# A one-core encoder layer: RWKV inverses solved in place through one scratch tensor, DVE block transposes, score pieces of four chunks, and stores issued by ACT

## The chip, the cores and the metric

The kernel runs on one core of a Trainium2 chip. A core has five engines that run at the same time, each with its own instruction stream in program order: TensorE (PE; PEld is its weight load), VectorE (DVE), ScalarE (ACT), GpSimd (POOL) and SyncE (SP). DMA transfers are issued by SP, by POOL or by ACT, and an instruction that issues one stands in that engine's queue like any other. The metric is the device time in microseconds of one execution.

## The reference

One layer of a "hybrid streaming encoder" on a prompt of 1,024 rows and a sample of 64 rows, width 1,024. One input projection of 9,864 columns feeds three token mixers and the gates:

```python
cols = x @ lw['w_in'] + lw['b_in']
ya, shift1, wkv1 = rwkv7_branch(a_cols, ...)     # A: 8 heads x 64, delta-rule state
yb, conv1, c1, n1, m1 = mlstm_branch(b_qk, ...)  # B: 4 heads x 128, matrix memory
yc = stick_breaking(c_q, kc, vc, k_past, v_past) # C: 8 heads x 64, attention without softmax
br = einsum('btnc,ncd->btnd', [ya*silu(a_z), yb*silu(b_z), yc*silu(c_z)], w_branch)
mix = sum(sigmoid(gates) * br, axis=2) @ w_out
x = layer_norm(DEEPNORM_ALPHA * x + mix)
x = x + (p @ w_ple) * sigmoid(x @ w_ple_gate)
```

Branch A is the recurrence `S = S*w_t + (S @ -kk_t) (kk_t*a_t)^T + v_t k_t^T`, `y_t = S @ r_t`. The kernel does it in chunks of 64 rows. Within a chunk the effect of the rows on each other is the inverse of a 64x64 unit triangular matrix, one for each head and chunk.

## The kernel before, in words

**Two kinds of work.** `main` computes the input projection in blocks of 128 columns, each in three row groups (384, 384, 320). A block is 72 matmuls: eight pieces of the inner dimension, three products each, since an fp32 number is split into two parts (`xh`, `xl` for x, `whl` for the weights). ACT or DVE evicts a group from one of three PSUM banks into one of four stages, and `store` writes the stage to DRAM (`xsd`, `brd`, `crd`, `bo`, `yz`, `gt`). The blocks stand in the order A, gates of B, B, C, then the silu and merge gates. `main` ends with `m_begin` (L1007), which waits until C is done and the first branch is converted for the merge (`m_prep`, `yconv`); then come the merge (three branches of eight blocks, `bk<-heapr,whl`) and the tail (`w_out`, layer norm, `w_ple`).

Beside it runs `side`: the three mixers one after the other. `a_all` does eight fronts (four pairs of heads, two halves of 8 and 9 chunks), `b_all` begins when the last front is done, and `c_all` when B is done. C's products have operands in the `heapr` buffer alone (`bk<-heapr`), and their evictions go to ACT and DVE.

**What sets the order.** A planner (`Sched`, L125) runs while the program is built. It keeps a clock for each engine and a price for each instruction, and takes a side task's next instruction as soon as its inputs are ready by these clocks; in between it emits `main`'s matmuls. The result is one fixed order for each engine. `get` (a piece of the heap) holds a task until the heap has room, and `bank` until a PSUM bank is free.

**The way of one RWKV half.** `a_front` (L1332) makes scores: `SC` holds, for each chunk, two 64x64 triangles (the one to invert, and the one for the output), `UV` the values; both are taken for the whole half and given back at the end of `a_chain`. At its end it writes the four 32x32 diagonal blocks of the pairs to the scratch `nd`, eight DMAs with 128-byte runs (L1480 to L1486). `a_inverse` (L1495) loads them as N, one block to a partition (two DMAs, 4 KB a partition), sets Q to the identity, and for j from 31 to 1 does two products on POOL: `tm = N[:, j] * Q[j, :]`, `Q -= tm`. DVE makes a transposed copy of the upper blocks in N (L1518), and Q and N go to the scratches `qd` and `xd`. `a_corner` (L1526) brings them back in ten DMAs with 128-byte runs, and makes the off-diagonal block of each inverse by two small products on TensorE (32x32, `bk<-heap,heap 32*32`) with ACT between. `a_chain` (L1573) then walks through the chunks one by one. Only one inverse and one corner run at a time.

All of these DMAs, the stores of `main` and the weight loads are issued by SP, in order.

## Time and profile before

| what | value |
|---|---|
| time, median of 3 runs | 1,891.88 us (1,881.05 to 1,899.76) |
| the profiled execution's own time | 1,887.65 us |
| its span, first to last instruction | 1,885.9 us |
| mean granted TensorE clock | 0.973 |
| POOL, DVE, ACT busy | 30%, 62%, 42% |
| DMA packets | 212,280, of them 41,592 under 512 B |

The profile is of one execution. The page has the busy time of each engine, the span in 40 slices of 47 us (a digit is tenths of busy time), the chain of work that ended last, and groups of instructions by line. Rows of a stretch give, for each engine, its busy time and in brackets the count of its instructions, then the granted clock (1.00 is full speed), the share of the DMA engines and GB/s. A row of a group reads: line, engine, operation, out<-in with shapes, count | busy us, mean ns of one | idle time before it and what ended it. Rows of DMA issues (`SPq`) give the least, median and largest time that the queue spent on one issue, and when the first and last began. A line such as L353, L358 or L427 is that of a helper (`act`, `tt`, `dma`) which many places call; in the changed kernel these below L384 are the same and the others four higher.

### The profile page before, as it was taken

The page shows a single profiled execution, that of the slowest core. Times are in us where ns is not written, and L with a number is a line of the kernel's source. Part 1 is how long each engine was busy: PE and PEld are TensorE (multiplying, and loading weights), DVE is VectorE, ACT ScalarE, POOL GpSimd, SP SyncE. Part 2 cuts the span into 40 slices and gives each one's busy share as a digit, 9 for nine tenths or more (in the row PEclk, how much of TensorE's full clock was granted, in tenths as well). Part 3 has the DMA queues.
Part 4 walks back from the last instruction along what each step waited for, and adds up shares of the span by engine and source line. Part 5 has one row for each costly group of instructions (what it writes and reads, how often), then busy time and mean ns, then how long its engine had stood idle before and what let it go on. Part 6 is the DMA issues. An engine that isn't in the chain of part 4 may idle for free.

```text
span 1885.9 us, 30250 instructions
## 1 busy us (share of the span) xinstructions
PE 1763.8 (94%) x10873; PEld 1619.1 (86%) x10873; DVE 1178.7 (62%) x2588; ACT 784.9 (42%) x1781; POOL 556.9 (30%) x1028
## 2 busy tenths in 40 slices
PE   6999999989999999999999999999966799988999
PEld 5999888979898899999999999999844799866787
DVE  8346466564647554756876266666666678888643
ACT  5444444344444344545444354645453222211321
POOL 6007445362617522810611221212020000345100
PEclk9999999999999999999999999999977899989999
DMA  4323423223232332343633442423211877522321
GB/s 148 109 83 87 112 71 95 80 83 109 77 92 67 110 85 77 99 119 114 198 122 115 141 125 68 116 90 110 72 53 35 264 229 232 158 90 78 125 80 60
DMA packets 212280, 206.55 MB, mean 110 GB/s; under 512 B 41592, under 2 KB 180650, under 8 KB 212130
## 3 DMA queue, kind: packets, MB, share of 16 engines
q1 hardware_dynamic: 207338, 191.86, 33.4%
q0 software_dynamic: 4704, 12.71, 2.1%
q8 instruction: 86, 1.41, 0.3%
q14 instruction: 64, 0.52, 0.1%
q10 hardware_dynamic: 88, 0.04, 0.0%
HBM read 136.25 MB, written 68.34 MB: 108 GB/s over the span
## 4 chain that ended last, share of the span: by engine, by line
PE 41%; issue 8%; DVE 8%; ACT 2%; POOL 2%; DMA 1%; SPq 0%; POOLq 0%; DVEq 0%; ACTq 0%
PE bk L321 39%; PE bk L328 3%; DVE heap L376 2%; DVE heap L397 2%; DVE heap L358 2%; DVE heapr L358 1%; POOL heap L414 1%; ACT heapr L353 1%; ACT heap L353 1%; DMA heap<-yz 1%; DMA heap<-gd 0%; DVE whl L358 0%; DVE heap L408 0%; POOL heap L419 0%; ACT whl L353 0%
## 5 line engine op out<-in xcount | busy, mean ns | idle before, releaser
L321 PE MATMUL bk<-xh,whl 128*128 128x384 f32 (+3 forms) x3792 | 1065.9, 342 | 0.3 <-DVE heap L376 0.3
L321 PEld LDWEIGHTS bk<-xh,whl 128*128 128x128 f32 (+1 forms) x3792 | 685.0, 188 | 11.9 <-issue 3.0
L321 PE MATMUL bk<-xl,whl 128*128 128x384 f32 (+3 forms) x2184 | 674.7, 330 | 1.7 <-POOL xl L360 1.2
L321 PEld LDWEIGHTS bk<-xl,whl 128*128 128x128 f32 (+1 forms) x2184 | 406.0, 189 | 6.0 <-POOL xl L360 1.8
L353 ACT ACTIVATE heap<-bk 64x64 f32<-64x64 f32 (+10 forms) x639 | 216.4, 346 | 433.1 <-PE bk L321 143.9
L360 POOL TENSOR_TENSOR heap<-heap 32x31 f32<-32x31 f32 (+33 forms) x514 | 347.0, 675 | 159.4 <-DMA heap<-nd 121.2
L328 PE MATMUL bk<-ident,heap 128*128 128x128 f32 (+3 forms) x942 | 184.7, 293 | 57.1 <-DVE heap L376 18.5
L358 DVE TENSOR_TENSOR whl<-heap,whl 128x1024 fp32r<-128x1024 f32 (+1 forms) x114 | 122.8, 1078 | 147.8 <-ACT whl L353 121.8
L328 PEld LDWEIGHTS bk<-ident,heap 128*128 128x128 f32 (+3 forms) x942 | 125.3, 149 | 82.3 <-DVE heap L376 21.4
L358 DVE TENSOR_TENSOR heap<-heap 128x256 f32<-128x256 f32 (+18 forms) x376 | 186.4, 501 | 13.6 <-DMA heap<-yz 2.8
L321 PE MATMUL bk<-heap,heap 128*128 128x128 f32 (+3 forms) x1360 | 170.6, 255 | 18.7 <-ACT heap L353 16.6
L321 PEld LDWEIGHTS bk<-heap,heap 128*128 128x128 f32 (+2 forms) x1360 | 142.9, 162 | 46.2 <-ACT heap L353 31.6
L353 ACT ACTIVATE heap<-bk,pc 128x384 f32<-128x384 f32 (+5 forms) x218 | 114.3, 547 | 137.4 <-PE bk L321 102.0
L321 PE MATMUL bk<-heapr 128*128 128x256 f32 (+2 forms) x524 | 131.0, 355 | 12.1 <-DVE heapr L358 5.6
L376 DVE SCALAR_TENSOR_TENSOR heap<-heap 128x4 f32<-128x4 f32 (+9 forms) x265 | 106.0, 402 | 50.4 <-ACT heap L353 45.0
L321 PE MATMUL bk<-heapr,whl 128*128 128x384 f32 (+2 forms) x648 | 119.6, 343 | 18.8 <-ACT heapr L353 18.5
L353 ACT ACTIVATE heap<-heap 64x64 f32<-64x64 f32 (+9 forms) x328 | 111.0, 343 | 61.5 <-DVE heap L376 20.1
L353 ACT ACTIVATE whl<-heap 128x1024 fp32r<-128x1024 f32 (+1 forms) x116 | 105.4, 910 | 68.0 <-PE bk L321 58.9
L321 PEld LDWEIGHTS bk<-heapr,whl 128*128 128x128 f32 x648 | 110.6, 192 | 25.2 <-ACT heapr L353 20.3
L321 PEld LDWEIGHTS bk<-heapr 128*128 128x128 f32 x524 | 89.4, 202 | 29.8 <-DVE heapr L358 12.1
L397 DVE TENSOR_TENSOR_SCAN heap<-heap,cst 128x128 f32<-128x128 f32 (+8 forms) x68 | 96.3, 1420 | 28.2 <-POOL heap L414 16.2
L353 ACT ACTIVATE heap<-bk,hb 128x384 f32<-128x384 f32 (+1 forms) x120 | 67.5, 563 | 109.5 <-PE bk L321 88.9
(153 smaller groups left out, 1808.4 us busy)
## 6 DMA issues: line engine op xcount, KB each, us to landing
heap<-in_w_in_dram SPq DMA_DIRECT2D x77, 512.0 KB
heap<-gt SPq DMA_DIRECT2D x24, 544.0 KB
gt<-heap SPq DMA_DIRECT2D x48, 192.0 KB
heap<-in_x_prompt_dram SPq DMA_DIRECT2D x16, 512.0 KB
heap<-crd SPq DMA_DIRECT2D x12, 544.0 KB
heap<-yd SPq DMA_DIRECT2D x24, 272.0 KB
heap<-yz SPq DMA_DIRECT2D x24, 272.0 KB
heap<-in_w_branch_dram SPq DMA_DIRECT2D x24, 256.0 KB
```

Of the source, the lines that this page charges most:

```text
L321: lambda: self.nc.tensor.matmul(out, lhsT, rhs, start=start, stop=stop, skip_group_check=more),
L328: lambda: self.nc.tensor.transpose(out, in_, self.ident[:p, :p]), load=(0.82 * fsize(in_), d))
L353: return self.nc.scalar.activation(out, in_, func, **kw)
L358: lambda: self.nc.vector.tensor_tensor(out=out, in0=a, in1=b, op=op))
L360: lambda: self.nc.gpsimd.tensor_tensor(out=out, in0=a, in1=b, op=op))
L376: lambda: self.nc.vector.scalar_tensor_tensor(out=out, in0=a, scalar=s, in1=b, op0=op0, op1=op1))
L397: return self.S.emit("dve", fsize(out) * 1.06 + 65, rd, [out], lambda: self.nc.vector.tensor_tensor_scan(out=out, data0=d0, data1=d1, init ...
L414: return self.S.emit("pool", fsize(out) * 1.0 + 130, [in_], [out], lambda: self.nc.gpsimd.affine_select(out=out, in_=in_, pattern=pattern, ...
```

## The change

Four edits, and one price in the planner:

1. **Pieces.** `SC` and `UV` are taken for four chunks at a time, and given back in `a_chain` as soon as the fourth chunk is through. The triangle to invert is stored with its sign turned (`maskb`), and its whole 64x64 form goes to `nd` as soon as four chunks are scored: four or five DMAs in a half, 256-byte runs, in place of eight.
2. **In place.** N is loaded from `nd` (two DMAs, 128-byte runs in the scratch), gets ones on its diagonal, and is inverted in place for j from 30 to 1; Q, its clearing and `qd`, `xd` are gone. The result goes back to the same places of `nd` (two DMAs).
3. **Block transposes.** `a_corner` fetches whole triangles in four or five DMAs in place of ten, and DVE transposes their upper blocks (`tr32`), in place of the copy on DVE and two loads from `xd`.
4. **Stores.** `raw`, which evicts the blocks of B and C, the output gate and the merge gates, has ACT issue the store right behind its own eviction. The silu blocks (`z`) and A's blocks keep SP.
5. The planner's price of a scan becomes 2.13 ns an element and 90, from 1.06 and 65.

```diff
-HEAP = 17256
+HEAP = 17264
+    def tr32(self, out, in_):
+        return self.S.emit("dve", fsize(out) * 1.06 + 65, [in_], [out], lambda: self.nc.vector.transpose(out, in_))
     def scan(self, out, d0, d1, init, op0, op1):
-        return self.S.emit("dve", fsize(out) * 1.06 + 65, rd, [out], lambda: self.nc.vector.tensor_tensor_scan(
+        return self.S.emit("dve", fsize(out) * 2.13 + 90, rd, [out], lambda: self.nc.vector.tensor_tensor_scan(
...
-            self.store(i_, dst[:, t0:t0 + n], d, done if g == 2 else None)
+            self.store(i_, dst[:, t0:t0 + n], d, done if g == 2 else None, kind != "z")
-    def store(self, i, out, d, done):
+    def store(self, i, out, d, done, now=False):
+        if now:
+            self.dma(out, d, "a")
+            if done:
+                self.have.add(done)
+            return
         self.kept |= {i}
...
-        inv = [self.must(n, True) for n in (1024, 1024, 256, 288)]
+        inv = [self.must(n, True) for n in (1024, 240, 288)]
+        yield self.cp(self.maskb, self.mask[:, :])
+        yield self.ts(self.maskb[:, 64:128], self.mask[:, 64:128], -1.0, OP.mult)
...
-        SC = yield from self.get(nc * 256)
-        UV = yield from self.get(nc * 128)
+        SC, UV = [], []
+        nd = self.dr.tile([9, 2, 64, 64], F32, name="nd", bufs=3)
         for c0 in range(0, nc, 4):
+            SC.append((yield from self.get(m * 256)))
+            UV.append((yield from self.get(m * 128)))
...
             for e in range(min(m, 2)):
+                yield self.dma(nd[c0 + e:c0 + m:2].rearrange("c h s j -> (h s) c j"),
+                               sc4[:, e::2, 0, 64 - 64 * e:128 - 64 * e], "s")
...
-        for k in range(2):
-            for h in range(2):
-                s = slice(64 * h + 32 * k, 64 * h + 32 * k + 32)
-                for e in range(2):
-                    o = 64 - 64 * e + 32 * k
-                    yield self.dma(nd[k, h * nc + e:(h + 1) * nc:2].rearrange("c s j -> s c j"),
-                                   sc4[s, e::2, 0, o:o + 32], "s")
...
+        blk = [nd.rearrange("c h s j -> (c h) s j")[0:B, 32 * k:32 * k + 32, 32 * k:32 * k + 32] for k in range(2)]
-            yield self.dma(N[k * B:(k + 1) * B, :1024], nd[k, 0:B].rearrange("c s j -> c (s j)"), "s")
-        yield self.memset(Q[0:P, :1024], 0.0)
-        yield self.memset(Q[0:P, :1024][:, ::33], 1.0)
+            yield self.dma(rows[k], blk[k], "s")
+        yield self.memset(N[0:P, :1024][:, ::33], 1.0)
-        for j in range(31, 0, -1):
-            w = 32 - j
+        for j in range(30, 0, -1):
+            w = 31 - j
             yield self.tt(t3, n3[:, 0:j, j:j + 1].to_broadcast([P, j, w]),
-                    q3[:, j:j + 1, j:32].to_broadcast([P, j, w]), OP.mult, IE)
-            yield self.tt(q3[:, 0:j, j:32], q3[:, 0:j, j:32], t3, OP.subtract, IE)
+                    n3[:, j:j + 1, j + 1:32].to_broadcast([P, j, w]), OP.mult, IE)
+            yield self.tt(n3[:, 0:j, j + 1:32], n3[:, 0:j, j + 1:32], t3, OP.add, IE)
-        yield self.cp(N[0:B, :1024].rearrange("p (j s) -> p j s", s=32),
-                Q[0:B, :1024].rearrange("p (s j) -> p j s", j=32))
         for k in range(2):
-            yield self.dma(qd[k, 0:B].rearrange("c s j -> c (s j)"), Q[k * B:(k + 1) * B, :1024], "s")
-        yield self.dma(xd[0:B].rearrange("c s j -> c (s j)"), N[0:B, :1024], "s")
+            yield self.dma(blk[k], rows[k], "s")
...
+                yield self.dma(v, nd[cs].rearrange("c h s j -> (h s) c j"), "s")
+        for v, cs in parts:
+            yield self.tr32(x13[:, cs, :], v[:, :, 0:32])
...
                 if c % 4 == 3 or c == 8:
+                    self.free(SC[c // 4], UV[c // 4])
-            self.free(BK, KR, PC, SC, UV)
+            self.free(BK, KR, PC)
```

How this moves instructions, at three places. First TensorE at the end of C, before: projections have `xh,whl`, C's products `heapr` or `ident,heap`, the merge `heapr,whl`. These are the last rows of C and the first of the merge:

```order
L328 MATMUL bk_69<-ident,heap 128x128 x4
L321 MATMUL bk_72<-heapr 128x256
L321 MATMUL bk_68<-heapr 128x256
L321 MATMUL bk_72<-heapr 128x256 x3
L328 MATMUL bk_70<-ident,heap 128x128 x4
L321 MATMUL bk_68<-heapr 128x256 x3
L321 MATMUL bk_72<-heapr 128x256 x4
L321 MATMUL bk_65<-heapr,whl 128x384 x12
```

The same place now, the last products of C:

```order
L321 MATMUL bk_65<-xh,whl 128x384
L321 MATMUL bk_72<-heapr 128x256
L321 MATMUL bk_65<-xh,whl 128x384
L321 MATMUL bk_65<-xl,whl 128x384
L321 MATMUL bk_65<-xh,whl 128x384
L321 MATMUL bk_72<-heapr 128x256 x3
L321 MATMUL bk_66<-xh,whl 128x384
L321 MATMUL bk_66<-xl,whl 128x384
```

Before, 298 products of C stand behind the last projection; now projections stand between them to the last, and 120 behind it.

Second SP around one inverse (the second half of the first pair), before:

```order
L427 DMA qd<-heap 18x1024 x2
L427 DMA xd<-heap 18x1024
L743 DMA heap<-in_w_in_dram 128x8x128
L427 DMA brd<-heap 128x320
L427 DMA heap<-xd 32x9x32
L427 DMA heap_76<-qd 32x5x32
L427 DMA heap<-bond 128x256
L427 DMA heap_76<-qd 32x4x32
L427 DMA heap_76<-qd 32x5x32
L427 DMA brd<-heap 128x384
L427 DMA heap_76<-qd 32x4x32
L427 DMA heap<-xd 32x9x32
```

Such a place now:

```order
L431 DMA nd<-heap 18x32x32
L431 DMA nd<-heap_76 128x2x64
L431 DMA nd<-heap 18x32x32
L431 DMA nd<-heap_76 128x2x64
L431 DMA heap<-nd 128x2x64 x3
L431 DMA heap_76<-xsd 128x576
L431 DMA heap<-nd 16x32x32
L431 DMA heap_76<-xsd 128x576 x2
L431 DMA yd<-heap 128x256
L431 DMA heap<-nd 128x2x64
L431 DMA heap<-nd 128x64
```

Two issues take an inverse out and five bring its triangles back, the next half's pieces and loads stand between, and no store of a projection block (`brd`) does.

Third ACT while C runs, with what each instruction waits for in brackets (`DMAHW4` is one of eight slots that DMAs take in turn), now:

```order
L353 ACTIVATE heap<-bk_66,hb 128x384 [waits DMAHW2_49,PE_49]
L431 DMA gt<-heap 128x384 [waits DMAHW4_49,Activation_49]
L353 ACTIVATE heap<-bk_68 128x128 [waits DVE_49,PE_49]
L353 ACTIVATE heap<-bk_70 128x128 [waits PE_49]
L353 ACTIVATE heap<-bk_71 128x256 [waits PE_49]
L353 ACTIVATE heap<-bk_69 128x256 [waits PE_49]
L353 ACTIVATE heap<-bk_67,hb 128x320 [waits DMAHW5_49,PE_49]
L431 DMA gt<-heap 128x320 [waits DMAHW6_49,Activation_49]
```

The store waits for ACT's own eviction and for an older transfer in its slot, and the evictions of C wait behind it; before, no DMA stood between them.

More of the change, by code (lines that the diff above doesn't have):

```diff
@@ L1315, in a_all @@
                "V2": self.must(128, True), "U2": self.must(128, True), "bn": [self.must(256, True) for _ in range(2)]}
-        inv = [self.must(n, True) for n in (1024, 1024, 256, 288)]
+        inv = [self.must(n, True) for n in (1024, 240, 288)]
         self.bkd = self.must(1024, True)
+        mb = self.must(192, True)
+        self.maskb = mb[:, :192]
+        yield self.cp(self.maskb, self.mask[:, :])
+        yield self.ts(self.maskb[:, 64:128], self.mask[:, 64:128], -1.0, OP.mult)
         lists = ("Z", "ya", "bn")
-        self.ast = [*Z, *cst["ya"], *cst["bn"], *[x for k, x in cst.items() if k not in lists], *inv, self.bkd]
+        self.ast = [*Z, *cst["ya"], *cst["bn"], *[x for k, x in cst.items() if k not in lists], *inv, self.bkd, mb]
         self.bond = self.dr.tile([4, 128, NT], F32, name="bond")
@@ L1451, in a_front @@
             for i, c in enumerate(cr):
-                yield self.stt(sc4[:, c, 0, :], bs[0][:, i * 128:(i + 1) * 128], nsb[:, c:c + 1],
-                               self.mask[:, c % 2 * 64:c % 2 * 64 + 128], OP.mult, OP.mult)
+                yield self.stt(sc4[:, i, 0, :], bs[0][:, i * 128:(i + 1) * 128], nsb[:, c:c + 1],
+                               self.maskb[:, c % 2 * 64:c % 2 * 64 + 128], OP.mult, OP.mult)
             for e in range(min(m, 2)):
-                yield self.tt(sc4[:, c0 + e:c0 + m:2, 1, :],
+                yield self.dma(nd[c0 + e:c0 + m:2].rearrange("c h s j -> (h s) c j"),
+                               sc4[:, e::2, 0, 64 - 64 * e:128 - 64 * e], "s")
+            for e in range(min(m, 2)):
+                yield self.tt(sc4[:, e::2, 1, :],
                               bs[1][:, :m * 128].rearrange("p (a b) -> p a b", b=128)[:, e::2, :],
@@ L1552, in a_corner @@
             for h in range(2):
-                yield self.mm(bs[h][top[h], c * 32:(c + 1) * 32], x13[low[h], c, :], sc4[low[h], c, 0, 96 - c % 2 * 64:128 - c % 2 * 64], True, True)
+                yield self.mm(bs[h][top[h], c * 32:(c + 1) * 32], x13[low[h], c, :], tri(c)[low[h], 32:64], True, True)
         for h in range(2):
-            for e in range(2):
-                yield self.act(sc4[top[h], e::2, 0, 96 - 64 * e:128 - 64 * e],
-                               bs[h][top[h], :nc * 32].rearrange("p (a b) -> p a b", b=32)[:, e::2, :], AF.Copy, scale=-1.0)
+            for v, cs in parts:
+                yield self.act(v[top[h], :, 32:64],
+                               bs[h][top[h], :nc * 32].rearrange("p (a b) -> p a b", b=32)[:, cs, :], AF.Copy)
             self.unbank(bs[h])
@@ L1599, in a_chain @@
             C0, nc_ = (0, 8) if hf == 0 else (8, 9)
-            bk3, kr3, sc4, uv3 = BK.v(nc_, 128), KR.v(nc_, 128), SC.v(nc_, 2, 128), UV.v(nc_, 128)
+            bk3, kr3 = BK.v(nc_, 128), KR.v(nc_, 128)
             for c in range(nc_):
+                sc3, uv2 = (x[c // 4].v(min(4, nc_ - c // 4 * 4), n, 128)[:, c % 4] for x, n in ((SC, 2), (UV, 1)))
+                uv2 = uv2[:, 0, :]
                 if c + C0 == 16:
```

51 lines of the change are left out of this document (24 added, 27 removed).

## The prediction

> **What bounds the kernel now.** I read the page from the top: the busy line, then the slices.
>
> ```profile
> span 1885.9 us, 30250 instructions
> PE 1763.8 (94%) x10873; PEld 1619.1 (86%) x10873; DVE 1178.7 (62%) x2588; ACT 784.9 (42%) x1781; POOL 556.9 (30%) x1028
> PE   6999999989999999999999999999966799988999
> ```
>
> TensorE is busy 94% of the span, so its work sets the time nearly everywhere, and a change to the RWKV branch (POOL, DVE, DMA) can only pay where TensorE is not covered. The slices show two such places before the tail: the start, and slices 29 to 31 (6, 6, 7), around 1,365 to 1,480 us. I then cut the time by stages with the busy time of the engines in chosen stretches:
>
> ```profile
> core 0: us, PE busy (x) PEld busy (x) DVE busy (x) ACT busy (x) POOL busy (x), PEclk, DMA share, GB/s
> 82.00:810.00 728.00, 701.10 (x4721) 654.71 (x4720) 418.12 (x1190) 321.06 (x842) 332.37 (x599) 0.99 0.32 90
> 810.00:1075.00 265.00, 262.47 (x1751) 251.16 (x1750) 166.55 (x483) 117.80 (x301) 62.67 (x128) 1.00 0.42 130
> 1075.00:1150.00 75.00, 73.25 (x467) 68.80 (x466) 49.31 (x56) 43.58 (x81) 17.21 (x48) 1.00 0.41 131
> 1150.00:1361.00 211.00, 206.06 (x1332) 194.38 (x1330) 139.06 (x158) 109.39 (x206) 31.17 (x108) 1.00 0.31 93
> 1361.00:1453.00 92.00, 63.45 (x309) 49.59 (x307) 63.33 (x77) 44.39 (x87) 13.83 (x45) 0.80 0.12 32
> 1453.00:1477.00 24.00, 5.73 (x10) 2.66 (x10) 10.79 (x15) 4.59 (x7) 0.00 (x0) 0.56 0.62 200
> 1477.00:1624.00 147.00, 146.93 (x874) 146.02 (x874) 112.10 (x204) 36.37 (x64) 2.17 (x4) 0.99 0.74 241
> ```
>
> From 82 to 1,361 us TensorE issues one matmul per 0.15 to 0.16 us and stands still for 36 us in all (26.9 + 2.5 + 1.8 + 4.9). From 1,361 to 1,477 it issues 319 in 116 us, at a granted clock of 0.80 and then 0.56. This is one hole, and why it opens is told by the last store of the projections and by who ended TensorE's waits there (first row the stores; the others the waits from 1,361 to 1,477):
>
> ```profile
> L427 SPq DMA_DIRECT2D gt<-heap x72: 319/320/562, 922.5 to 1361.4; - x72
> ```
> ```profile
> PE bk L321 <- ACT heapr L353: 23.6, 14, 6.8
> PE bk L328 <- DVE heapr L358: 10.6, 2, 5.3
> ```
>
> The last projection block leaves at 1,361 us. Until then stick-breaking attention (C) runs between projection matmuls, which fill its waits. After it, 298 products of C stand in TensorE's order with nothing between them (the first excerpt of the order in the section on the change), so each wait for an eviction or a split is bare. Then comes the conversion of the first branch for the merge, bare as well:
>
> ```profile
> 1451.89 0.62 PE L321 MATMUL bk<-heapr 128*128 128x256 f32 x3 [0.34 <-DVE heapr L358]
> 1459.30 1.77 PE L321 MATMUL bk<-heapr,whl 128*128 128x384 f32 x3 [6.79 <-ACT heapr L353]
> ...
> 1476.36 2.09 PE L321 MATMUL bk<-heapr,whl 128*128 128x384 f32 x4 [3.98 <-ACT heapr L353]
> ```
>
> So the bound is TensorE's work plus one hole of 116 us, which exists because C starts too late for the projections to last.
>
> **The main term: C starts earlier.** The change itself does no TensorE work less; counted in the built order, both kernels have 7,984 products ahead of the merge, 5,616 of them projections. What moves is the mixture. Before, 3,471 projection matmuls stand ahead of the last corner product of the RWKV inverses, 4,704 ahead of C's first product, and all 5,616 ahead of its last 298. Now it is 2,517, 3,963, and 5,496 ahead of C's last product: 120 are left behind it. The fronts wait for heap; score pieces that are freed after four chunks let them in sooner, and mLSTM and C follow. The planner's new price for a scan also moves C's rows; it is nearer to the trace, where a scan of 1,024 took 2,277 ns, about 2.2 ns an element:
>
> ```profile
> L397 DVE TENSOR_TENSOR_SCAN heap<-heap,cst 128x1024 f32<-128x1024 f32 x8 | 18.2, 2277 | 0.0
> ```
>
> What do 319 products cost when they are covered? In 1,150 to 1,361 the two mixtures run together:
>
> ```profile
> L321 PE MATMUL bk<-xh,whl 128*128 128x384 f32 (+1 forms) x506 | 143.7, 337 | 0.0
> L321 PE MATMUL bk<-xl,whl 128*128 128x384 f32 (+1 forms) x253 | 83.0, 328 | 0.0
> ```
>
> 506 + 253 = 759 of the 1,332 are projections. A dense row of such matmuls costs 147/874 = 0.168 us (the stretch from 1,477). 759 x 0.168 = 127.5 us; the other 573 products share the remaining 83.5 us, 0.146 us each. The hole holds 309 of C and 10 of the merge: 309 x 0.146 + 10 x 0.168 = 46.8 us. So 116 us become 47: **-69 us**. The smallest saving is where the 69.2 us of busy time there (63.45 + 5.73) do not shrink at the full clock: -47. The largest takes all C products at 0.13 us: -74. I take -69, since the interleaved stretch is the same code doing the same steps.
>
> **What is late next.** The conversion for the merge needs C's buffers free, so it still starts after C. It took from 1,452.5 to 1,477, 24.5 us. The 120 projections behind C cover 120 x 0.168 = 20.2 us, but they bring evictions to ACT and weight splits to DVE, which do the conversion too. I put back **+8 us**: between 24.5 - 20.2 = 4 and half as much again for the conversion, 36.7 - 20.2 = 16.
>
> **The inverse.** Per half it has 60 POOL products instead of 62, over 4,960 elements each way instead of 5,456 (the sums over j of j(31-j) and j(32-j)), and one clearing of 1,024 less.
>
> ```profile
> L360 POOL TENSOR_TENSOR heap<-heap x496: 227/592/2531, 146.8 to 793.9; 32x31 f32<-32x31 f32 x6, 32x112 f32<-32x112 f32 x6, 32x175 f32<-32x175 f32 x6, 32x220 f32<-32x220 f32 x6
> ```
> ```profile
> 466.80:508.20 41.40, 36.50 (x62) 1.00 0.21 64
> 741.20:794.10 52.90, 46.27 (x62) 1.00 0.30 88
> ```
>
> The fifth inverse took 41.4 us of POOL, the last 52.9. At 4,960/5,456 of the work the typical one takes about 38. Eight follow each other on POOL (8 x 38 = 304 us); from the first inverse to the last corner the new order has some 2,440 products (3,524 less 1,087, counted to the corners), at 0.154 us 376 us. That is enough, though with less room. Two small DVE instructions make the negated mask before the branch begins. The copy that transposed one triangle on DVE goes (eight of some 1.1 us), and 36 block transposes come:
>
> ```profile
> L381 DVE COPY heap<-heap 18x1024 f32<-18x1024 f32 x4 | 4.4, 1096 | 0.5 <-POOL heap L360 0.5
> L381 DVE COPY heap<-bk 64x64 f32<-64x64 f32 x68 | 14.8, 218 | 35.5 <-PE bk L321 34.9
> ```
>
> The trace has no block transpose. With 64 elements in a lane it is nearest to the copy of 64 (0.22 us, 8 us in all); like the long copy it would be 39 us. I take 0.22: nothing, since DVE stands idle 43% of 82 to 810 us. Without that cover it is four or five in a row, 1 us, ahead of each corner.
>
> The transfers around an inverse all stand in SP's queue:
>
> ```profile
> L427 SPq DMA_DIRECT2D nd<-heap x64: 302/432/1736, 124.2 to 735.9; - x64
> L427 SPq DMA_DIRECT2D heap<-nd x16: 281/360/1284, 141.2 to 737.7; - x16
> L427 SPq DMA_DIRECT2D heap<-qd x64: 303/431/697, 203.0 to 815.6; - x64
> L427 SPq DMA_DIRECT2D qd<-heap x16: 296/360/413, 198.1 to 794.5; - x16
> L427 SPq DMA_DIRECT2D heap<-xd x16: 303/394/622, 202.4 to 803.3; - x16
> L427 SPq DMA_DIRECT2D xd<-heap x8: 264/300/370, 199.0 to 795.3; - x8
> ```
>
> 184 issues become 104 (36 pieces out, 16 blocks in, 16 back, 36 pieces in). 80 x 0.43 = 34 us of SP's issuing go, 4 us per half. But the blocks now go in and out in runs of 32 numbers (128 B) where they went in runs of 4 KB. Landing can be bounded by the two kinds: 4 KB runs, issued at 144.04 and used by POOL at 146.82; 128 B runs, issued at 215.91 and used by TensorE at 217.96:
>
> ```profile
> 144.04 0.38 SPq L427 DMA_DIRECT2D heap<-nd  x1
> ```
> ```profile
> 146.82 1.33 POOL L360 TENSOR_TENSOR heap<-heap 32x31 f32<-32x31 f32 x4 [6.14 <-DMA heap<-nd]
> ```
> ```profile
> 215.91 0.58 SPq L427 DMA_DIRECT2D heap<-qd  x1
> ```
> ```profile
> 217.96 0.69 PE L321 MATMUL bk<-heap,heap 32*32 32x32 f32 x32
> ```
>
> 2.8 and 2.05 us: no price for the short runs shows. I take 0 net for the inverse, between -4 and +6 us per half of its own latency, which TensorE does not wait for while its order leaves the room.
>
> **Stores from ACT.** 156 stores of 128x384 leave SP (24 blocks of B and C, 28 of two gate kinds, three each). On ACT each costs its issue and a wait for ACT's own eviction to be written (and, in the order, for an older transfer in its slot). The nearest row:
>
> ```profile
> L427 ACTq DMA_DIRECT2D grd<-heap x6: 246/250/271, 208.6 to 217.9; - x6
> ```
>
> 0.25 to 0.32 us (SP's `gt` stores) and as much again for the wait: 156 x 0.5 = 78 us on an ACT that is idle half of 1,150 to 1,361 (109 of 211). Behind a store stand the evictions of C and RWKV, for which TensorE waits, so up to a quarter may show: 0 to +15 us. Against it SP, freed of them, issues loads sooner. I take **0** for ACT and for the denser RWKV stage together, between -8 and +20.
>
> **Sum**, on the profiled execution's own 1,887.65 us (1.75 above its span, 4 below the median of the three runs): 1,887.65 - 69 + 8 = **1,826 us**.
>
> **The rivals.**
> (a) POOL is late: the RWKV stage gets denser, and every inverse runs like the last one (52.9 instead of 41.4). For: that row. Against: TensorE's waits from 82 to 1,361 us name no DMA; the longest is
>
> ```profile
> PE bk L321 <- ACT heap L353: 18.4, 25, 2.2
> ```
>
> and the other four name DVE. If half of the 11.5 us shows at eight corners, 8 x 5.7 = 46: 1,872. The Trainium skill, in "SBUF — State Buffer", section "Who interferes with whom", says that a POOL instruction that reads SBUF and a DVE instruction with two SBUF inputs exclude each other for a whole instruction; the one long inverse would fit that, and no run here isolates it.
> (b) Short runs cost: two 2 us legs more per inverse, bare on TensorE, 8 x 4 = 32: 1,858. Against: the 2.05 us above. The Trainium skill, in "DMA: Bandwidth & Descriptors", section "Specifications", asks for 512 B or more to a piece and says that smaller ones are read, changed and written back; by it (b) would hold, and the trace shows no such price at these counts.
> (c) The hole only moves: C's own chain is slow wherever it runs, and TensorE waits in order among projections. Against: 206 of 211 us busy in 1,150 to 1,361. Then 1,880 to 1,888.
> (d) Slower: ACT stands still at each store until an older transfer lands. A group of projections lasts 24 x 0.168 = 4.0 us; ACT uses 109/211 of it, so 1.9 us are free. A hold of 2.0 to 2.8 us and 0.3 to issue exceeds that by 0.4 to 1.2, say 0.8: 156 x 0.8 = 125, 1,951. It decides from 61/156 = 0.4 us lost per store. Against: the six stores of `grd` that ACT issues now at 0.25 us.
>
> **How the numbers follow.** The forecast 0.80 (its own range 1,800 to 1,850), (a) 0.06, (b) 0.04, (c) 0.05, (d) 0.05. The range, 1,800 to 1,862, spans the forecast's with -74 and the gains in SP at the lower end and reaches over (b). More than 1% is about what a measurement of this kernel can tell from no change. Faster by more: the forecast, (b) and half of (a), 0.87. Within 1%: the rest of (a) and most of (c), 0.08. Slower: (d), 0.05.
>
> **What would show it.** Right: `gt` stores end within some 25 us of C's last product; TensorE's slices at 29 to 31 read 9; granted clock near 1.0 to the merge; one wait of under 15 us before it. POOL products 480, the last inverse done about 120 us earlier. Wrong: TensorE's still time from 82 us to C's end above 60 us, with POOL, DMA or ACT as its releaser; ACT's queue standing over 1 us at stores.

## The result, and the profile after

The changed kernel took 1,791.7 us (median of four runs, 1,787.4 to 1,796.0) beside 1,892.6 us for the kernel before: a ratio of 0.947, 95% interval 0.942 to 0.953. The forecast was 1,826 us, with 1,800 at the lower end of its range. The direction and the place were right; the gain was half as large again as the forecast. The profiled execution took 1,793.5 us, 94 less than the 1,887.65 on which the sum was made, where the forecast was 62 less.

The page of the changed kernel, its span, the busy line of TensorE, the slices and POOL's products:

```profile
span 1791.5 us, 30062 instructions
PE 1719.0 (96%) x10873; PEld 1591.3 (89%) x10873; DVE 1169.2 (65%) x2618; ACT 790.8 (44%) x1821; POOL 511.3 (29%) x1004
PE   6999999999999999999999999999998999978999
L360 POOL TENSOR_TENSOR heap<-heap 32x30 f32<-32x30 f32 (+16 forms) x498 | 312.3, 627 | 37.3
```

TensorE has as many matmuls as before (10,873) and the hole of slices 29 to 31 (counted from 0) is gone: they read 9, 8, 9. Next the stretches, cut where the built order changes: RWKV up to its last chain, mLSTM up to the first product of stick-breaking (C), C among projections, the conversion for the merge, and the rest. No product of C is left without projections, so the bare stretch of before has no counterpart.

```profile
81.00:713.00 632.00, 609.68 (x4266) 555.32 (x4264) 414.81 (x1275) 311.47 (x893) 292.28 (x579) 1.00 0.34 95
713.00:951.00 238.00, 237.31 (x1542) 230.39 (x1542) 149.57 (x421) 111.07 (x258) 48.91 (x116) 1.00 0.44 136
951.00:1353.00 402.00, 402.00 (x2648) 389.19 (x2648) 257.14 (x295) 214.91 (x395) 71.46 (x209) 1.00 0.34 99
1353.00:1389.00 36.00, 29.93 (x167) 28.63 (x166) 15.03 (x22) 10.49 (x18) 0.00 (x0) 0.91 0.72 231
1389.00:1791.00 402.00, 374.99 (x1874) 327.66 (x1872) 282.75 (x495) 100.75 (x182) 67.70 (x41) 0.97 0.43 140
```

From 81 us to C's end TensorE stands still for 22.3 + 0.7 + 0.0 = 23 us. The third row is the surprise: 2,648 products in 402 us without any idle time. The same cut through the kernel before:

```profile
1087.00:1361.00 274.00, 267.31 (x1725) 251.21 (x1722) 183.16 (x209) 144.64 (x277) 47.70 (x153) 1.00 0.33 99
```

There 6.7 us were idle, and a product took 274/1,725 = 0.159 us; now 0.152. The other places that the prediction named, in the changed kernel: the stores of the gates, the waits of TensorE from 1,353 us, the block transposes, and POOL's products of the inverses.

```profile
L431 ACTq DMA_DIRECT2D gt<-heap x72: 326/326/379, 952.4 to 1373.7; - x72
```
```profile
PE bk L321 <- ACT heapr L353: 5.7, 2, 5.1
PE bk L321 <- DVE heapr L376: 0.3, 1, 0.3
```
```profile
L386 DVE STREAM_TRANSPOSE heap<-heap x36: 163/230/246, 197.3 to 650.5; 128x64 f32<-128x64 f32 x32, 128x32 f32<-128x32 f32 x4
```
```profile
120.00:720.00 600.00, 264.72 (x480) 1.00 0.34 97
```

The last store goes 20 us after C's last product, one wait of 5.1 us stands ahead of the merge, a transpose takes 0.23 us, and POOL does 480 products in 264.7 us, 33 us per half.

### The profile page after: what moved, and what is told of

Same layout as the page of the kernel before. It is cut to its first block, busy times and chain, and to the rows that moved or that the text cites. A ratio compares the mean times of both kernels' runs of the same rounds, so it can differ in the third digit from the quotient of the medians.

```text
span 1791.5 us, 30062 instructions
## 1 busy us (share of the span) xinstructions
PE 1719.0 (96%) x10873; PEld 1591.3 (89%) x10873; DVE 1169.2 (65%) x2618; ACT 790.8 (44%) x1821; POOL 511.3 (29%) x1004
## 3 DMA queue, kind: packets, MB, share of 16 engines
q0 software_dynamic: 4704, 12.71, 2.2%
## 4 chain that ended last, share of the span: by engine, by line
PE 81%; DVE 11%; ACT 4%; issue 2%; DMA 2%; ACTq 0%; SPq 0%; POOL 0%; DVEq 0%
PE bk L321 76%; PE bk L328 6%; DVE heap L376 4%; ACT heap L353 3%; DVE heap L358 2%; DVE heap L371 1%; DVE heapr L358 1%; DVE whl L358 1%; DVE heap L412 1%; DMA heap<-in_x_prompt_dram 1%; DVE xl L358 0%; DMA heap<-in_w_ple_dram 0%; DMA out_c_p_dram<-heap 0%; DVE heap L409 0%; ACT whl L353 0%
## 5 line engine op out<-in xcount | busy, mean ns | idle before, releaser
L321 PEld LDWEIGHTS bk<-xh,whl 128*128 128x128 f32 (+1 forms) x3792 | 681.1, 187 | 13.5 <-issue 3.9
L353 ACT ACTIVATE heap<-bk 64x64 f32<-64x64 f32 (+9 forms) x679 | 219.2, 335 | 399.9 <-PE bk L321 137.8
L360 POOL TENSOR_TENSOR heap<-heap 32x30 f32<-32x30 f32 (+16 forms) x498 | 312.3, 627 | 37.3
L328 PE MATMUL bk<-ident,heap 128*128 128x128 f32 (+3 forms) x942 | 177.3, 280 | 36.4 <-DVE heap L376 22.1
L358 DVE TENSOR_TENSOR heap<-heap 128x256 f32<-128x256 f32 (+15 forms) x359 | 176.1, 497 | 16.2 <-DMA heap<-yz 7.8
L358 DVE TENSOR_TENSOR whl<-heap,whl 128x1024 fp32r<-128x1024 f32 (+1 forms) x114 | 121.7, 1069 | 91.2 <-ACT whl L353 87.9
L321 PE MATMUL bk<-heap 128*128 128x128 f32 (+6 forms) x1156 | 169.0, 270 | 10.0 <-ACT heap L353 8.5
L328 PEld LDWEIGHTS bk<-ident,heap 128*128 128x128 f32 (+3 forms) x942 | 120.7, 143 | 55.0 <-DVE heap L376 25.8
L321 PEld LDWEIGHTS bk<-heap 128*128 128x128 f32 (+2 forms) x1156 | 126.6, 163 | 40.6 <-ACT heap L353 21.9
L353 ACT ACTIVATE heap<-heap 64x64 f32<-64x64 f32 (+8 forms) x328 | 111.0, 343 | 63.4 <-DVE heap L376 30.5
L376 DVE SCALAR_TENSOR_TENSOR heap<-heap 128x4 f32<-128x4 f32 (+8 forms) x264 | 100.8, 383 | 55.3 <-ACT heap L353 49.6
L401 DVE TENSOR_TENSOR_SCAN heap<-heap,cst 128x512 f32<-128x512 f32 (+8 forms) x68 | 96.4, 1419 | 45.5 <-POOL heap L418 26.1
L321 PE MATMUL bk<-heapr 128*128 128x256 f32 (+2 forms) x524 | 119.4, 329 | 0.0
L321 PE MATMUL bk<-heap,heap 128*128 128x128 f32 (+3 forms) x788 | 108.2, 263 | 8.3 <-ACT heap L353 6.5
```

The lines of the kernel that those rows point to most:

```text
L321: lambda: self.nc.tensor.matmul(out, lhsT, rhs, start=start, stop=stop, skip_group_check=more),
L328: lambda: self.nc.tensor.transpose(out, in_, self.ident[:p, :p]), load=(0.82 * fsize(in_), d))
L353: return self.nc.scalar.activation(out, in_, func, **kw)
L358: lambda: self.nc.vector.tensor_tensor(out=out, in0=a, in1=b, op=op))
L360: lambda: self.nc.gpsimd.tensor_tensor(out=out, in0=a, in1=b, op=op))
L376: lambda: self.nc.vector.scalar_tensor_tensor(out=out, in0=a, scalar=s, in1=b, op0=op0, op1=op1))
```

## The experiments

Twelve kernels were run, in three sets; the kernel before took 1,890.7, 1,890.8 and 1,889.0 us beside them. "Bare" are C's products behind the last projection, "behind" the projections behind C's last product, both counted in the built order (the traces hold some of C's products as two records, so that 298 bare ones are 310 there). "Idle" is TensorE's idle time in the stretch of C among projections and in the conversion; "per product" is the length of the first by its count of products.

| kernel | time, us | ratio (95%) | bare / behind | idle in C's mixed part / conversion, us | per product, us |
|---|---|---|---|---|---|
| before | 1,890 | 1 | 298 / 0 | 6.7 / 18.3 | 0.159 |
| in-place inverse alone | 1,823.5 | 0.963 (0.958 to 0.967) | 43 / 0 | 10.2 / 18.8 | 0.158 |
| + pieces | 1,820.4 | 0.961 (0.957 to 0.966) | 0 / 474 | 13.5 / 0 | 0.159 |
| + scan price | 1,812.1 | 0.959 (0.955 to 0.962) | 68 / 0 | 0 / 18.8 | 0.151 |
| + pieces, price | **1,781.6** | 0.941 (0.936 to 0.945) | 0 / 186 | 0 / 0.1 | 0.152 |
| + pieces, half the price | 1,789.1 | 0.946 (0.944 to 0.949) | 0 / 354 | 0 / 0 | 0.151 |
| + pieces, ACT stores | 1,811.3 | 0.956 (0.950 to 0.961) | 0 / 378 | 12.3 / 0 | 0.159 |
| + price, ACT stores | 1,851.0 | 0.980 (0.976 to 0.983) | 233 / 0 | 0 / 20.4 | 0.151 |
| all of the change | 1,791.7 | 0.947 (0.942 to 0.953) | 0 / 120 | 0 / 6.1 | 0.152 |
| 1st order, stores by SP | 1,788.9 | 0.947 (0.944 to 0.949) | 0 / 120 | 1.6 / 7.9 | 0.152 |
| 2nd order, stores by ACT | 1,786.1 | 0.946 (0.942 to 0.950) | 0 / 186 | 0 / 0 | 0.152 |
| in-place alone, heap held | 1,823.1 | 0.965 (0.962 to 0.968) | 0 / 21 | 11.0 / 16.6 | 0.159 |
| in-place alone, old work added | 1,873.9 | 0.991 (0.988 to 0.995) | 179 / 0 | 10.0 / 19.0 | 0.159 |
| the price alone | 1,919.7 | 1.016 (1.013 to 1.018) | 484 / 0 | 0 / 18.9 | 0.153 |

Rows with "+" contain the in-place inverse with its single scratch tensor and its transposes; the first and second order are those of the changed kernel and of the 1,781.6 us one. The last two rows lie within 2% of the kernel before, though their intervals exclude 1. One column sorts all fourteen kernels: with the old price a product takes 0.158 to 0.159 us, with the new or the half-way one 0.151 to 0.153. The share of projections differs between them and does not make this: with each projection taken off at 0.168 us, the other products take 0.147 to 0.151 us in the six kernels with the old price and 0.128 to 0.131 in the eight others (counted in the traces from C's first product to its last, or to the last projection).

### Parts of the change

**In-place inverse alone.** Against the changed kernel, scores are whole again, stores go by SP, the scan has its old price. Of the first edit it keeps one part: whole triangles go to the scratch as soon as four chunks are scored. So does every kernel with a "+" and the two at "in-place alone". Its edit, cut (`...`):

```diff
-        return self.S.emit("dve", fsize(out) * 2.13 + 90, rd, [out], lambda: self.nc.vector.tensor_tensor_scan(
+        return self.S.emit("dve", fsize(out) * 1.06 + 65, rd, [out], lambda: self.nc.vector.tensor_tensor_scan(
-            self.store(i_, dst[:, t0:t0 + n], d, done if g == 2 else None, kind != "z")
+            self.store(i_, dst[:, t0:t0 + n], d, done if g == 2 else None, False)
...
+        SCw = yield from self.get(nc * 256)
+        UVw = yield from self.get(nc * 128)
...
-            SC.append((yield from self.get(m * 256)))
-            UV.append((yield from self.get(m * 128)))
+            SC.append(Buf(SCw.heap, SCw.off + c0 * 256, m * 256))
+            UV.append(Buf(UVw.heap, UVw.off + c0 * 128, m * 128))
...
-                    self.free(SC[c // 4], UV[c // 4])
...
-            self.free(BK, KR, PC)
+            self.free(BK, KR, PC, *self.whole.pop((p, hf)))
```

> The in-place inverse with whole triangles and block transposes alone: score pieces are taken and freed for the whole half as before, SP issues all stores, the planner's scan price is the old one. Counted in the built order, 43 of C's products stand behind the last projection (298 before, 0 with the whole change). Theory 1, the hole alone decides: each product of C that is no longer bare saves about 0.17 us (92 us for 309 against 0.13 us each), the bare conversion for the merge stays: 1888 - 255 x 0.17 = 1845 us, between 1835 and 1855. Rival, the score pieces do most of the work: nearer to before, 1870 to 1890.

Measured: 1,823.5 us, 67 less than before: the largest part of the whole gain, from an edit that the prediction costed at nothing. It is 11.5 us below theory 1's range. Beside the hole, TensorE's idle time in the RWKV stage fell by 10 us, from 26.9 to 17.1.

**In-place inverse and pieces** (the first two pairs of lines above, scores in pieces).

> Pieces and in-place inverse, but SP issues all stores and the planner's scan price is the old one. No product of C is bare, and 474 projections stand behind C, so the conversion is covered too. Theory 1, the hole alone: as fast as the whole change or some 6 us faster, 1786 to 1796 us. Theory 2, the scan price takes waits of some 14 us out of the mixed part of C, where TensorE waits for the DVE work behind the scans: 1797 to 1810, with TensorE idle 6 us or more in C's mixed part and the wait of L328 for DVE L358 back.

Measured: 1,820.4 us, 10 above theory 2's range; both of theory 2's signs are there (13.5 us idle in the mixed part, 7.5 of them L328's waits for DVE L358). The pieces bring the last corner and C forward by far more than was missing, but only 3 us come of it: 474 projections are left behind C, more than the conversion needs (the kernel with all but the stores from ACT, below, covers it with 186).

**All but the price** (the first pair alone).

> The whole change with the old scan price. 378 projections stand behind C. Theory 1 (hole alone): 1786 to 1796 us. Theory 2 (the scan price also takes waits out of C's mixed part): 1797 to 1810. That ACT's stores cost something: as slow as the whole change plus theory 2's 14 us, and slower than the kernel with pieces and in-place inverse alone.

Measured: 1,811.3 us, 1 above theory 2's range. So the price by itself, in an otherwise finished change, is worth 20 us. The last sentence of the expectation fails: with the old price the kernel with stores from ACT is 9 us faster than the one without (1,806.9 to 1,812.5 against 1,815.6 to 1,827.7). Its waits in C's mixed part, and its stretches:

```profile
PE bk L328 <- DVE heap L358: 5.5, 7, 1.3
PE bk L321 <- DVE heapr L358: 4.7, 10, 1.8
PE bk L328 <- DVE heapr L358: 1.5, 2, 1.3
PE bk L321 <- DVE heap L358: 0.2, 1, 0.2
```
```profile
960.00:1341.00 381.00, 368.72 (x2395) 346.35 (x2394) 251.79 (x291) 204.58 (x382) 69.08 (x205) 1.00 0.32 94
1341.00:1409.00 68.00, 68.00 (x417) 68.00 (x416) 20.13 (x27) 20.70 (x33) 0.84 (x4) 1.00 0.57 181
```

11.9 of 12.3 us idle end with a DVE product. In the changed kernel the same list is empty from 951 to 1,353 us. Of these 20 waits, 15 end with a DVE product that stands directly behind a scan in DVE's stream, and the other five within three instructions of one. One of them, first DVE, then TensorE:

```profile
1014.48 2.02 DVE L401 TENSOR_TENSOR_SCAN heap<-heap,cst 128x896 f32<-128x896 f32 x1
1016.41 0.67 DVE L358 TENSOR_TENSOR heapr<-bk,heapr 128x512 fp32r<-128x512 f32 x1
```
```profile
1017.13 0.74 PE L321 MATMUL bk<-heapr 128*128 128x256 f32 x4 [0.58 <-DVE heapr L358]
```

The second row of the stretches is the conversion with enough projections beside it: no idle time at all.

**All but the stores from ACT** (the second pair alone).

> The whole change with every store back on SP. 186 projections stand behind C. Theory 1: 1786 to 1792 us (the conversion after C is covered by 31 us of projections). If ACT's stores relieve SP and this feeds TensorE: slower than the whole change by 5 us or more, with SP waiting for ACT again. If ACT's stores cost 0.1 us each on TensorE: faster by some 15 us, 1775 to 1780.

Measured: 1,781.6 us (1,778.8 to 1,785.7), the fastest kernel of the study, faster than the whole change (1,787.4 to 1,796.0). It lies between the expected ranges, 1.6 us above the one in which ACT's stores cost TensorE time. Its conversion:

```profile
1343.00:1380.00 37.00, 36.86 (x227) 36.62 (x226) 15.81 (x23) 11.69 (x20) 0.21 (x1) 1.00 0.69 220
```

With 186 projections behind C it stands still for 0.1 us, where the changed kernel, with 120, stands for 6.1.

### The price of a scan

**The price alone,** on the kernel before:

```diff
-        return self.S.emit("dve", fsize(out) * 1.06 + 65, rd, [out], lambda: self.nc.vector.tensor_tensor_scan(
+        return self.S.emit("dve", fsize(out) * 2.13 + 90, rd, [out], lambda: self.nc.vector.tensor_tensor_scan(
```

> The kernel before, with one line changed: the planner's price of a scan is 2.13 ns an element plus 90 instead of 1.06 plus 65. Stick-breaking is planned slower, so in the built order 484 of its products stand behind the last projection instead of 298 (with the old in-place-less inverse the pieces are still whole). Theory 1 (only the bare rows count; before, 298 bare rows took 92 us where covered ones take 0.13 to 0.15 each, so a bare row costs about 0.17 us more): 186 more bare rows, +32 us, about 1,920 to 1,925 us. Theory 2 (the true price also takes the waits for DVE out of the mixed part, worth 20 to 39 us in the runs with the in-place inverse): +32 less 20 to 28, 1,895 to 1,905; TensorE's idle time and its excess over the dense rate in the mixed part, 6.7 and 28.0 us before, fall to near 0 and below 20. Theory 3 (the price by itself is what made the kernel faster, whatever the hole): below 1,880.

Measured: 1,919.7 us.

```profile
1106.00:1330.00 224.00, 224.00 (x1466) 217.28 (x1464) 135.62 (x160) 118.60 (x221) 38.62 (x117) 1.00 0.35 105
1330.00:1481.00 151.00, 104.42 (x506) 80.75 (x505) 108.20 (x125) 68.95 (x136) 29.74 (x81) 0.80 0.13 38
```

The total is that of theory 1 (0.3 us below its range), and theory 2's range is missed; but theory 2's sign is there: no idle time is left in the mixed part, and a product takes 0.153 us. The bare part eats more than that up: 151 us where the kernel before had 92. Theory 3 falls: without room behind it the better price makes the kernel slower, by 1.6%.

**Half the price,** with pieces and SP's stores (`fsize(out) * 1.6 + 90`).

> The kernel with all of the change but the stores from ACT, and a scan priced half way: 1.6 ns an element plus 90. In the built order 354 projections stand behind stick-breaking, against 474 with the old price (1,820.4 us) and 186 with the new one (1,781.6). Theory D (dose: the planner puts a scan's readers too early by what the price lacks of the measured 2.2 ns an element, and TensorE stands for them): half of the 39 us, 1,796 to 1,806, with 4 to 8 us idle in the mixed part against 13.5 and 0. Theory L (any other order would have done, the gain is the luck of one order): no such place between them; 1,780 to 1,785 or 1,815 to 1,825. Theory C (fewer projections behind the end of stick-breaking are what counts): 1,820.4 - 120 x 39/288 = 1,804, with the excess in the mixed part as with the old price.

```profile
952.00:1317.00 365.00, 364.96 (x2417) 351.31 (x2416) 251.72 (x291) 204.59 (x382) 68.00 (x206) 1.00 0.35 100
```

Measured: 1,789.1 us, below the range of the dose theory and above that of a lucky order. The waits are gone already at 1.6 ns an element, so the effect is no straight line; it has a step somewhere between 1.06 and 1.6. Nor do the fewer projections behind C explain it: the rate per product falls as soon as the waits go. That the rate is the luck of one order is ruled out by the table: all eight orders with the new or the half-way price have it, and none of the six with the old one.

**The price with whole scores,** SP's stores.

> The kernel with the in-place inverse alone, whole scores and stores on SP (1,823.5 us), and the new price of a scan; with the pieces it would be the 1,781.6 us kernel, so it completes a square of pieces and price, whose other corner is 1,820.4. Theory S (sum: the price is worth 39 us wherever it is put, pieces 3): 1,784. Theory I (each spends what the other gives: the price spreads stick-breaking over more projections, and the pieces are what provides these): 68 bare rows in the built order against 43, so 25 x 0.17 = +4, and the waits for DVE gone from the mixed part, -17: 1,806 to 1,815, with the 20 us of the conversion still bare. Theory B (only bare rows count): 1,828.

Measured: 1,812.1 us, theory I. It closes a square: 1,823.5 with neither pieces nor price, 1,820.4 with the pieces, 1,812.1 with the price, 1,781.6 with both. Alone they bring 3 and 11 us, together 42.

**The change without its pieces,** all else as changed.

> The changed kernel (1,791.7 us) with scores and values kept whole for a half as before; all else of the change stands. Built, 233 products of stick-breaking are bare, where the changed kernel has none and 120 projections behind. Theory I (pieces provide the room that the price and the stores then use): 233 x 0.17 = 40, and the conversion bare again, about 13 more than the changed kernel's 6: 1,838 to 1,848. Theory S (pieces are worth the 3 us that they were worth alone): 1,793 to 1,798.

```profile
1340.00:1412.00 72.00, 51.04 (x243) 39.11 (x241) 50.76 (x60) 29.46 (x60) 10.44 (x40) 0.81 0.07 18
1412.00:1446.00 34.00, 13.62 (x46) 10.30 (x46) 14.47 (x22) 6.78 (x11) 0.00 (x0) 0.60 0.64 205
```

Measured: 1,851.0 us, 3 above theory I's range. In the full change the pieces are worth 59 us, though they were worth 3 without price and stores: 72 us of bare C and 20 us idle in the conversion come back.

### Why the in-place inverse is early

**Its heap taken away.** The in-place inverse alone, with 856 columns held:

```diff
         inv = [self.must(n, True) for n in (1024, 240, 288)]
+        ballast = self.must(856, True)
```

> The kernel with the in-place inverse and the single scratch tensor alone (1,823.5 us; 43 bare rows), with 856 columns of the heap held through the RWKV stage and freed with its other state: what the in-place inverse gives back of the heap is taken away again. Theory H (the in-place inverse is early because it leaves heap to the next front): the lead is lost, stick-breaking stands bare again as before, above 1,870 us. Theory W (it is early because a half's chain has less to issue and to multiply): the lead stays. The built order has no bare rows and 21 projections behind stick-breaking, so 43 x 0.17 = 7 us less for the bare rows and 3 for the covered part of the conversion: 1,812 to 1,823.

Measured: 1,823.1 us, as without it. The heap that the in-place inverse gives back is not the cause (theory H falls); theory W's range is met at its upper edge.

**The old amount of work.** The in-place inverse alone, with the transfers of pieces cut in two and idle work beside each inverse:

```diff
-                yield self.dma(v, nd[cs].rearrange("c h s j -> (h s) c j"), "s")
+                for h in range(2):
+                    yield self.dma(v[64 * h:64 * h + 64], nd[cs, h].rearrange("c s j -> s c j"), "s")
...
+        yield self.memset(q[0:P, :1024], 0.0)
+        yield self.tt(tm[0:P, :240], N[0:P, :240], N[0:P, 240:480], OP.mult, IE)
+        yield self.tt(q[0:P, :240], N[0:P, :240], tm[0:P, :240], OP.add, IE)
...
+        yield self.cp(q[0:B, :1024].rearrange("p (j s) -> p j s", s=32),
+                N[0:B, :1024].rearrange("p (s j) -> p s j", j=32))
```

The transfers out to the scratch are cut in the same way, and the two products are done twice.

> The kernel with the in-place inverse and the single scratch tensor alone, given back the old amount of work beside it: each transfer of pieces is cut in two (by head: 176 issues on SP for 104), and each inverse clears a scratch of 1,024, makes four further products of 240 on POOL and one further copy of 1,024 on DVE, into numbers that nobody reads. Theory W (fewer issues and less POOL work in a half's chain bring the last corner forward, and the bare rows follow): the built order has the last corner after 3,390 projections (before 3,471, in-place alone about 2,930) and 179 bare rows; 1,823.5 + 136 x 0.17 = 1,847 us, 1,840 to 1,855. Theory X (the gain is of the triangles' form itself, without the old transposed copy's late transfer, and not of the amounts): within 1,818 to 1,830.

Measured: 1,873.9 us, theory W's direction, and 19 us above its range. Its extra scratch holds 1,024 columns of heap, where 856 did no harm in the kernel above. How early the inverses are done is told by the start of their last POOL product. Before it was 793.9 us (the row stands in the prediction). Here are the rows of the in-place inverse alone, with its heap held, and with the old work:

```profile
L360 POOL TENSOR_TENSOR heap<-heap x480: 225/560/2623, 142.4 to 711.4; 32x58 f32<-32x58 f32 x8, 32x130 f32<-32x130 f32 x8, 32x184 f32<-32x184 f32 x8, 32x220 f32<-32x220 f32 x8
```
```profile
L360 POOL TENSOR_TENSOR heap<-heap x480: 227/556/3662, 142.2 to 705.7; 32x58 f32<-32x58 f32 x8, 32x130 f32<-32x130 f32 x8, 32x184 f32<-32x184 f32 x8, 32x220 f32<-32x220 f32 x8
```
```profile
L360 POOL TENSOR_TENSOR heap<-heap x512: 227/572/2631, 148.7 to 797.1; 32x240 f32<-32x240 f32 x11, 36x240 f32<-36x240 f32 x10, 32x58 f32<-32x58 f32 x6, 32x130 f32<-32x130 f32 x6
```

The lead of 82 us stays when the heap is taken away and is gone when the work comes back. Rows of the RWKV stage and of the bare part, first of the in-place inverse alone, then with the old work:

```profile
81.00:800.00 719.00, 701.88 (x4864) 652.51 (x4863) 436.85 (x1342) 340.89 (x957) 297.55 (x584) 0.99 0.33 95
1379.00:1389.00 10.00, 7.02 (x42) 5.14 (x40) 4.57 (x7) 3.85 (x9) 0.00 (x0) 1.00 0.07 23
```
```profile
81.00:886.00 805.00, 768.48 (x5203) 712.12 (x5202) 469.31 (x1371) 361.23 (x991) 335.18 (x628) 0.99 0.32 92
1392.00:1440.00 48.00, 35.92 (x193) 28.43 (x192) 34.14 (x38) 20.69 (x43) 6.41 (x17) 0.82 0.04 10
```
```profile
PE bk L321 <- ACT heap L353: 20.2, 36, 2.3
```

The bare part is 48 us where the in-place inverse alone had 10. The rest is in the RWKV stage: 36.5 us idle against 17.1, and the waits for ACT in the last row are 20.2 us where that kernel has 5.2. So the work of a half counts twice: by where the planner puts the last corner, and by TensorE waiting on the way. Given back together, issues and products undo 50 of the 67 us. The other 17 stay open; whole triangles written out early, for one, are in this kernel too. Which of the two does more stays open as well: in the built orders the in-place inverse alone has its last corner after 3,066 projections by the count used in the prediction (the 2,930 of the expectation was counted otherwise), 3,141 with the cut transfers alone, 3,105 with the extra work alone, and 3,390 with both, so they do not simply add; the single ones were not timed.

### Stores: the engine or the order

**The changed kernel's order, stores issued by SP.** The planner still books them as ACT's:

```diff
-            self.dma(out, d, "a")
+            self.dma(out, d, "A")
-        q = {"g": self.nc.gpsimd, "s": self.nc.sync, "a": self.nc.scalar}[e]
+        q = {"g": self.nc.gpsimd, "s": self.nc.sync, "a": self.nc.scalar, "A": self.nc.sync}[e]
-                           {"g": "pool", "s": "s", "a": "act"}[e])
+                           {"g": "pool", "s": "s", "a": "act", "A": "act"}[e])
```

> The changed kernel in the order that it has on every engine, with one difference: the stores that ACT issues are planned as ACT's, and are issued by SP at the same place of the order. So it has the changed kernel's 120 projections behind stick-breaking. The changed kernel takes 1,791.7 us, the one that is planned with SP's stores 1,781.6. Theory E (ACT loses the 10 us by issuing: 156 issues of 0.33 us and the waits ahead of them): 1,780 to 1,784. Theory O (the 10 us come from the order which the planner makes when the stores cost SP nothing): 1,789 to 1,794, with a wait of 5 to 6 us ahead of the merge as in the changed kernel.

**The 1,781.6 us kernel's order, stores issued by ACT** (the mirror of that edit).

> The other corner of the square: the order of the kernel whose stores SP issues (1,781.6 us; 186 projections behind stick-breaking), with the stores issued by ACT at the same places of the order. Theory E (issuing costs ACT the 10 us): 1,789 to 1,794. Theory O (the order costs them): 1,779 to 1,784. If both halves count, both this run and its partner lie between, near 1,786.

Measured: 1,788.9 and 1,786.1 us. The order with 120 projections behind C takes 1,791.7 by ACT and 1,788.9 by SP; the order with 186 takes 1,786.1 and 1,781.6. The engine is worth 3 to 4.5 us, no more than the scatter of one kernel's runs; the order 5.7 to 7.3, and it has a place in the trace, the conversion of the SP version of the first order and of the ACT version of the second:

```profile
1348.00:1386.00 38.00, 30.11 (x163) 28.82 (x163) 14.98 (x22) 10.52 (x18) 0.00 (x0) 0.87 0.68 219
```
```profile
1347.00:1384.00 37.00, 37.00 (x230) 37.00 (x229) 15.59 (x22) 12.04 (x21) 0.21 (x1) 1.00 0.76 233
```

The first order leaves 7.9 us idle there (6.1 when ACT issues), the second none (0.1 when SP issues). So mostly theory O, with this place as its evidence more than the times: between the two kernels with ACT's stores the 5.7 us are also within the scatter. And the order decides even the sign: with the old price, stores from ACT came with a kernel 9 us faster.

## Why the prediction was wrong in its size

**The failed step** is in the main term: "the other 573 products share the remaining 83.5 us, 0.146 each", and "I take -69, since the interleaved stretch is the same code doing the same steps". The code is the same, but 0.146 us held waits for DVE, and the change removes them with the price of a scan, of which the prediction said only that it "moves C's rows" and is "nearer to the trace". The same division for the mixed part now, with the rows of its projections:

```profile
L321 PE MATMUL bk<-xh,whl 128*128 128x384 f32 (+1 forms) x1055 | 295.7, 336 | 0.0
L321 PE MATMUL bk<-xl,whl 128*128 128x384 f32 (+1 forms) x528 | 172.5, 327 | 0.0
```

1,583 x 0.168 = 266 us of the 402; the other 1,065 products share 136 us, 0.128 each. In the kernel that lacks only the price they are 1,327 projections, and the other 1,068 products take 0.148. So the price saves 0.020 us on each of some 1,065 products, 21 us, and not on the 309 of the hole alone; for the others the prediction had no term. Measured between these two kernels: 20 us. How the price does it, by the trace: the idle time that ended with a DVE product behind a scan, 11.9 us, is gone. The rest lies in what the profile counts as busy, since a product counts 0.27 to 0.34 us there while most start 0.12 to 0.17 us apart: from the start of a projection to that of a product of C behind it the kernel without the price takes 0.248 us in the mean (181 times), the changed one 0.167 (200 times). The Trainium skill, in "DVE: opcode table, instruction layouts, handler registers and perf-mode slots", section "Datapath and trigger behaviour", says that this scan runs at half throughput; the trace agrees, with 2,277 ns for 1,024 elements against 1,096 for a copy of as many, and the old price, 1.06 ns an element, was about the copy's.

**The sum again.** The hole at 0.128 instead of 0.146: 309 x 0.018 = 5.6 us more, -75. C's other products, some 750 that were mixed already: 750 x 0.018 = -13.5. The conversion +6 where +8 was put back. TensorE's idle time in the RWKV and mLSTM stages, 29.4 us before and 23.0 now: -6.4. Together -89, of 94 measured; 5 us are not assigned, about the scatter of one kernel's runs.

**The hole** was read rightly: it closes because C starts earlier. What makes C early was read only in part. The prediction gave it to the score pieces ("score pieces that are freed after four chunks let them in sooner") and the inverse nothing. In the traces C's first product stands behind 4,704 projections before, 4,344 with the in-place inverse alone and 3,954 with the pieces too, so each does about half; but the first half leaves only 43 of the 298 bare products. Most of that half goes with the inverse's fewer issues and products, and none with its heap. This did not move the forecast, which counted the order that has both; so the fair size of the term says nothing for the reason given. The prediction took the inverse's "own latency" as harmless, since TensorE does not wait for it; but it is a link in the chain from one half to the next, and that chain sets where C starts.

The waits of POOL for its blocks from the scratch would not have told this. They are 121 us before and 148 in the in-place inverse alone, which is 67 us faster; in the changed kernel they are 54. (In-place, they stand at the instruction that writes the diagonal, L423, and no longer at the products.)

```profile
POOL heap L360 <- DMA heap<-nd: 121.2, 8, 24.7
```
```profile
POOL heap L423 <- DMA heap<-nd: 148.1, 8, 34.4
```
```profile
POOL heap L423 <- DMA heap<-nd: 54.3, 7, 18.5
```

**Point by point.** Conversion: +8 put back, 6.1 us idle, right. Block transposes: 0.22 us taken, 0.23 measured. POOL: 38 us for an inverse from its first product to its last, where the trace has 36 to 44, 40 in the mean. The busy time in it is 264.7/8 = 33 us; before it was 298.9/8 = 37.4, in this row:

```profile
120.00:820.00 700.00, 298.94 (x496) 0.99 0.32 91
```

Stores on ACT with the denser RWKV stage: 0 taken; in the full change the stores cost 10 us, of which 3 to 4.5 by issuing and the rest by the order, inside the stated -8 to +20. The last store and the single wait came as said; the granted clock is 1.00 up to the conversion and 0.91 in it. The last inverse ends at 630 us where it ended at 794, more than the 120 us named.

**The rivals.** (a) POOL late: no, the inverses take 36 to 44 us and not 52.9, and TensorE's idle time in the stage fell. (b) Short runs cost: no wait of TensorE in the RWKV stage of the changed kernel names a DMA. (c) The hole moves: no. (d) ACT stands at the stores: no, each of the 156 begins 0.03 us behind ACT's eviction, and the longest issue of a `gt` store takes 0.38 us, below the 0.4 lost per store from which it would decide.

## What to carry to other kernels

A wrong price in a planner costs where the order is tight, and shows as waits of the bottleneck engine in a stretch that is otherwise dense; check each priced instruction against its row in the trace, and apply what is won to every product of that kind, not only to those that move. Two edits that each bring little may bring much together: one spends the cover (later C), the other supplies it (earlier start), and either is worth nothing beyond what the next stretch can use. An engine off the critical path can still be a link of the chain that decides when the next stage starts: ask what one pass through that chain costs, and what begins later for it; its waits alone do not tell.

## What the runs showed of the hardware

Moving the 156 block stores from SP to ACT in one and the same order changed the time by 3 and 4.5 us, no more than the scatter of one kernel's runs: at most some 0.03 us a store, against the 0.33 us that one takes to issue. The granted clock was lower where TensorE's work was thin for long: 0.80 to 0.82 in the four bare stretches of 48 us and more (69 to 75% busy), 0.56 to 0.60 in the conversion without projections (24 to 43% busy), 1.00 in the same conversion with 186 of them or more. The bare stretch of 10 us in the in-place inverse alone, 70% busy, still had 1.00. The scan took 2.08 times as long as a copy of as many elements (2,277 and 1,096 ns for 1,024).
